# DeltaNet scan: one full product with zero-padded 128x128 q-k blocks in place of a pair of 64-column products

## The chip, the cores and the metric

The kernel runs on one core of a Trainium2 chip. The core has five engines with queues of their own: TensorE (PE in the profile, its weight loads PEld), VectorE (DVE), ScalarE (ACT), GpSimd (POOL) and SyncE (SP), which here only issues transfers. Each engine takes its instructions strictly in the order of its queue and waits at an instruction whose input or buffer isn't ready. Products land in PSUM, eight banks of 128 partitions x 512 fp32 numbers; all else lives in SBUF.

The metric is the device time of one execution in microseconds (us), smaller is better.

## What is computed

One layer of an encoder for two sequences with the same weights, 256 and 512 tokens, 1024 features, fp32 throughout. A modulated RMS norm gives `h`; one input projection feeds two mixers, neighbourhood attention with 8 heads of 64 and a gated DeltaNet with 4 heads of 128 that runs forward and backward; their outputs go through one output projection, then a second norm and a gated feed-forward with a convolution of width 3 follow. The change is in the DeltaNet, which works on chunks of 64 tokens:

```python
intra = jnp.where(causal, jnp.einsum('bhncd,bhnsd->bhncs', q, k) * decay, 0.0)
...
def step(S, xs):
    q_i, k_i, u_i, w_i, a_i, gl_i = xs
    v_new = u_i - jnp.einsum('bhcd,bhde->bhce', w_i, S)
    o = jnp.einsum('bhcd,bhde->bhce', q_i, S) + jnp.einsum('bhcs,bhse->bhce', a_i, v_new)
    S = S * jnp.exp(gl_i)[..., None, None] + jnp.einsum('bhcd,bhce->bhde', k_i, v_new)
    return S, o
```

`a_i` is `intra`, the masked 64x64 q-k matrix of a chunk; `a_i v_new` is the term that the change computes in another way.

## The kernel before

**Order of the work.** The kernel is traced as one long program of tiles. A framework then lays out the queue of every engine by priority (program order, with some parts raised) and by when it reckons that inputs and buffers are free, and it sets all waits. Tiles with the same tag share a fixed number of buffers (`bufs`); a tile whose buffer still has readers waits for them. So the order on an engine isn't written out by hand, and a change of buffers can change it.

**Stages.** The times are of the profiled execution. Norm and the first projections run up to about 73 us. The DeltaNet works on two pairs of heads (`hp` 0 and 1). For each pair there are projections (`dn_proj`, products on L476), the decay matrices (`dn_decay`: `rd` on L615 and L616, three products on L620, L621, a mask on POOL on L628), the q-k and k-k matrices (`dn_gram`), an inverse of 64x64 triangular blocks (`dn_solve`) and the scan (`dn_scan`). The first scan stands between 196 and 277 us, the second solve between 244 and 319, the second scan between 326 and 408. Beside the scans PE works off projections that don't depend on them: the second pair's, the gate `z` (both L476), and those of the attention (L868). The attention's core follows up to about 583, then the output projection, and from about 600 to the end the feed-forward, which neither uses nor feeds anything of the scan directly.

**Gram.** `dn_gram` writes the masked q-k matrices to `Ic` (L649), two 64x64 matrices for each pair of chunks: `[128, head, chunk pair, x, 64]`, rows 0 to 63 of one chunk, rows 64 to 127 of the other, one chunk of the forward and one of the backward direction.

**A step of the scan** (`step`, L752 to L806) does one chunk of both directions at once, for one head `j` and one sequence `s`. A scan has 8 + 4 steps in a row for two heads, 24 in all; the four rows (two heads, two sequences) are interleaved. One PSUM bank `B_` holds the three results of a step: `ps1` (256 columns), `ps2` and `ps4` (128 each). In order:

- L768: two products of `KQ` with the state `S` into `ps1`.
- L774 (DVE) makes the right side `r` of both halves, L781 (ACT) the part `tm` of the output. In the first step POOL copies `r` instead (L777).
- L782: the product with the inverse `Wbd` into `ps2`; this is `v_new`.
- L786 (DVE) and L788 (ACT) write scaled halves into `XS`.
- L790 (ACT), twice: each half of `ps2` is copied to its own 128-column part of `XB`, whose other rows are zero.
- L793: two products of `Kt` with `XS` into `ps1`; L796 (DVE) updates `S`.
- L802, twice: `Ic` (128 rows, 64 columns) times each part of `XB` into one half of the partitions of `ps4`.
- L806 (DVE) adds `tm` and writes the output over `Wbd`.

Instructions of different engines on the same PSUM bank are kept apart by waits, so L793, which writes the bank that L790 reads, comes after the copies.

**Other names that the steps below touch.** `MO` is a buffer of 6 KB a partition, used by constants at the start and by both solves (memset L657, copies L678, products L729, copies L735). `raw` (L875) holds the attention's queries or keys while they are normed (copies from PSUM L878, squares L884, a DVE chain from L885 to L888, transposes L894); it has one buffer, which `rd` shares. `zz` (L824) is a load into the buffer that the solve's products L729 read. The streams of the modulation use products with 32 columns (L192), and their weights go into `aw` and `au` (L502). `WRB` = 2 is the number of buffers for the loads of `w_o` (L1063). `vec` holds small per-feature vectors, among them the 176 columns for the feed-forward's convolution. L1224 are subtractions on POOL in the second norm.

Of the kernel before, what the change touches and what calls it, by code (L numbers as in the profile page):

```python
# [45 lines left out]
NV1 = VEC["n1g"][0]  # L46
NC1 = CST["bo"][0]
# [55 lines left out]
def layer(ctx: ExitStack, tc: tile.TileContext, I: dict, yout: bass.AP, dbg=None):  # L103
# [7 lines left out]
    vec = cpool.tile([P, VEC["_n"][1] - NV1], F32, name="vec")  # L111
# [3 lines left out]
    nc.sync.dma_start(vec[:], I["vec"][:, NV1:])  # L115
    nc.scalar.dma_start(cst[:], I["cst"][:, NC2:])

    vec2 = []

    def V(n, i=0, m=None):  # L120
        o, w = VEC[n]
        t_, o = (vec, o - NV1) if o >= NV1 else (vec2[0], o)
        return t_[:, o + i:o + (i + m if m is not None else w)]
# [14 lines left out]
    def load_w(pool, src, bufs, hp=HPW):  # L138
        """[128, 1024] weights -> (hi, lo)"""
# [11 lines left out]
    def rsqrt(out, v, shape, tag):  # L151
        """out = v ** -0.5 (v > 0), Newton on the integer seed"""
        a = small.tile(shape, F32, name="rs_a", tag="rs_a" + tag, bufs=2)
        ti = small.tile(shape, I32, name="rs_t", tag="rs_t" + tag, bufs=2)
# [23 lines left out]
    bw = cpool.tile([P, KD, 32], F32R, name="bw")  # L178
    braw = arow[:, 0:128].rearrange("p (k c) -> p k c", k=KD)
    nc.scalar.dma_start(braw, I["wba"])  # L180
    split(braw, bw[:, :, 0:16], bw[:, :, 16:32])

# [4 lines left out]
    def ada_piece(s, i, row, brow, load, PS, w4=None):  # L187
        """rows k = 4 i.. of set s; the four partial sums in rows 32 k.."""
        w4 = w4 or load(ada_src(s, i))
        p_ = PS()  # L190
        for kk in range(4):
            nc.tensor.matmul(p_[32 * kk:32 * kk + 32, :], cs[:, 4 * i + kk, :], w4[kk], start=True, stop=True)  # L192
        nc.vector.tensor_tensor(row[:], p_[:], row[:] if i else brow, ALU.add)
# [21 lines left out]
    def ada_ahead(sets, row, bias, load, PS):  # L215
        """each piece is loaded a step before it is used"""
# [24 lines left out]
    # ================= mixer =================  # L241
    with ExitStack() as mx:
# [20 lines left out]
        with tc.tile_pool(name="st", bufs=1, reuse_waits="tile") as st:  # L263
# [13 lines left out]
            # x, features on partitions  # L277
# [7 lines left out]
            # rstd of the tokens, along the free axis  # L285
# [50 lines left out]
            # the first four products run along with the rows of h  # L336
# [32 lines left out]
        at = px.enter_context(tc.tile_pool(name="at", bufs=1, side="right", reuse_waits="tile"))  # L369
# [14 lines left out]
        def gates_dn():  # L384
# [13 lines left out]
            ba = dn.tile([P, NT, 16], F32, name="ba")  # L398
# [3 lines left out]
            def to_slots(dst, src):  # L402
                """src [P, t, (d h)] -> dst [P, h, t', d]"""
# [10 lines left out]
            beta = dn.tile([P, 4, NT, 2], F32, name="beta")  # L414
            to_slots(beta, e1[:])
            y1 = dn.tile(sc8, F32, name="y1")
            nc.vector.tensor_tensor(y1[:], ba[:, :, 8:16], V("dtb").unsqueeze(1).broadcast_to(sc8), ALU.add)
            y2 = dn.tile(sc8, F32, name="y2")
# [4 lines left out]
            na = dn.tile([P, 8], F32, name="na")  # L423
            nc.scalar.activation(na[:], V("alog"), AF.Exp)
            nc.vector.scalar_tensor_tensor(y1[:], y1[:], -1.0, na[:].unsqueeze(1).broadcast_to(sc8), ALU.mult, ALU.mult)
            gg = dn.tile([P, 4, NT, 2], F32, name="gg")
# [16 lines left out]
            pdec = dn.tile(s48, F32, name="pdec")  # L443
# [18 lines left out]
        nc.gpsimd.memset(XB[:], 0.0)  # L462
# [21 lines left out]
        def ada_bufs():  # L484
            """buffers that the heads have left: five for weights, one for the bias row"""
# [3 lines left out]
            for tag, shape in (("dec", [P, 24, 64]), ("MO", [P, 12, P])):  # L489
                a_ = dn.tile(shape, F32, name="au", tag=tag)[:].rearrange("p a b -> p (a b)")  # L490
# [5 lines left out]
        def ada_load(src):  # L496
            """four k of a set"""
# [85 lines left out]
        def dn_scales(hp, sqs):  # L583
            # sums of squares: natural for k, swapped halves for q
# [6 lines left out]
            rkk = dn.tile([P, 2, NT], F32, name="rkk", tag="rkk", bufs=2)  # L591
# [40 lines left out]
        def dn_gram(hp, KQ, pp, dec, dv, SD):  # L632
            Ic = dn.tile([P, 2, NT, 2, 64], F32, name="Ic", tag="Ic", bufs=2)
            nc.vector.tensor_tensor(dec[:], dec[:], pp[:].rearrange("p h t d -> p (h t d)").unsqueeze(2).broadcast_to([P, 24, 64]), ALU.mult)
            dp = dec[:].rearrange("p (h t d) c -> p h t d c", h=2, t=NT)
            # Gram products
            for j in range(2):
                for b, n in SEQS:
# [6 lines left out]
                    for d in range(2):  # L645
                        ts_ = slice(0, n) if d == 0 else rev(0, n)
                        for e in range(2):
                            r_ = slice(e * 64, e * 64 + 64)
                            nc.vector.tensor_tensor(Ic[r_, j, b:b + n, e if d == 0 else 1 - e, :],  # L649
# [4 lines left out]
        def dn_solve(hp, Ic, dec, dv, SD):  # L654
            """operands [inverse of (1 + lower)] of every chunk; lhsT form, block-diagonal"""
# [23 lines left out]
            # one 32-block per partition (chunk, direction); upper form for both directions; its two blocks of 16  # L679
# [14 lines left out]
            # back to rows on partitions, as they are and transposed  # L694
# [9 lines left out]
            # blocks of 16 to blocks of 32  # L704
# [20 lines left out]
            def level(sel):  # L725
                """MO times the inverse (or its transpose), forward and backward"""
# [20 lines left out]
        def dn_scan(hp, KQ, Kt, Vt, pex, Ic, Wbd):  # L747
# [1 line left out]
            S = [[dn.tile([P, 2, P], F32, name=f"S{s}{j}", tag=f"S{s}{j}") for j in range(2)] for s in range(2)]  # L749
            half = lambda e: slice(e * 64, e * 64 + 64)  # L750

            def step(s, i, j):  # L752
# [8 lines left out]
                r = dn.tile([P, P], F32, name="r", tag="r", bufs=2)  # L761
                tm = dn.tile([P, P], F32, name="tm", tag="tm", bufs=2)
                xb = XB[:, j]
# [25 lines left out]
                for e in range(2):  # L789
                    nc.scalar.copy(xb[half(e), e, :], ps2[half(e)])  # L790
                if i < N - 1:
# [7 lines left out]
                    else:  # L799
                        nc.vector.tensor_copy(St[:].rearrange("p d c -> p (d c)"), ps1)  # L800
                for e in range(2):
                    nc.tensor.matmul(ps4[half(1 - e)], Ic[:, j, tp, x, :], xb[:, e, :], start=True, stop=True)  # L802
# [18 lines left out]
        def dn_final(hp, O, ssq):  # L821
# [1 line left out]
            zz = big.tile([P, 2, T], F32, name="zz", tag="sv")  # L823
            nc.sync.dma_start(zz[:], zd[2 * hp:2 * hp + 2].rearrange("h p t -> p h t"))  # L824
            so = dn.tile([P, 12], F32, name="so", tag="so")
            fo = dn.tile([P, 12], F32, name="fo", tag="fo")
# [31 lines left out]
        def att_proj(blk, evac):  # L858
            """token-major block of 256 columns; evac(psum tile with two token tiles, first t)"""
# [14 lines left out]
        def att_qk(hf, which, QT):  # L874
            raw = at.tile([P, NT, 4, 64], F32, name="raw", tag="raw", bufs=1)  # L875
# [4 lines left out]
            s_ = at.tile([P, 24], F32, name="s_", tag="s_")  # L880
            f_ = at.tile([P, 24], F32, name="f_", tag="f_")
            for i in range(24):
                jk = at.tile([P, 64], F32, name="jk", tag="jka", bufs=1)
# [35 lines left out]
        def att_core(hf, qk, SA, MX, units):  # L919
# [7 lines left out]
            # units of two query tiles: (query column, key blocks of kT, V tiles)  # L927
# [91 lines left out]

        def take(g, n):  # L1020
# [11 lines left out]
        pTs = [dn.tile([P, 512], F32, name="pT", tag=t)[:] for t in ("XS", "XB")]  # L1032
        scs = []
        for _ in range(2):
            sc3 = dn.tile([P, 3, 512], F32, name="sc", tag="Ic", bufs=2)
            scs.extend(sc3[:, u] for u in range(3))
# [43 lines left out]
        def proj(t, hd, pt, m, ks, tmp):  # L1080
            """X2 += gate * (rows ks of w_o)"""
# [9 lines left out]
        def proj_a():  # L1091
            """all but the last quarter of the mixer's columns"""
# [10 lines left out]
        def proj_b(t, raw, m, PS, tmp):  # L1103
            """the rest, the row's 1 / rms"""
# [31 lines left out]
    # ================= output projection, second norm =================  # L1136
    with ExitStack() as fx:
# [3 lines left out]
        dps = fx.enter_context(tc.tile_pool(name="dps", bufs=2, space=PSUM, reuse_waits="tile"))  # L1141
        h2hi = fp.tile([P, KD, T], F32R, name="h2hi")
# [231 lines left out]
```

## Time and profile before

| | |
|---|---|
| runs shown | 1191.91, 1193.77, 1193.95 us, median 1193.77 |
| profiled execution | span of 1191.6 us from the first to the last instruction, 17540 instructions; no time of its own is listed beside the span |
| mean granted TensorE clock | 0.981 |
| DVE, ACT, POOL busy | 726.8, 539.0, 69.0 us |
| DMA | 110.98 MB, mean 93 GB/s |
| L802, product `Ic` x `XB` | 192 weight loads of 136 ns and 192 product records of 273 ns (medians), from 200.4 to 407.2 us |
| L790, copies into `XB` | 96, median 261 ns |

An fp32 product appears as two records, one for each of its passes. A row of the timeline has its start, the time from its start to its end, engine, line, operation, what it writes and reads, the shape, how many instructions were merged, and in brackets the idle time before it and what ended that. "issue" is idle time in which the engine waited for nothing that the profile shows. Products overlap, so the busy time of PE is not the time for which it is held; for that the distances between starts are read.

### The profile page before, as it was taken

To read this page: it belongs to the slowest core of one execution; us is meant where nothing else is said; L and a number is where in the kernel's file an instruction comes from. 1 tells how busy PE (TensorE), PEld (TensorE's weight loads), DVE (VectorE), ACT (ScalarE), POOL (GpSimd) and SP (SyncE) were. 2 spreads that over 40 slices of the span, in tenths; PEclk is the share of its full clock that TensorE was granted. 3 is DMA by queue.
4 is the path that set the end of the run, shared out by engine and by line. 5 is a ranking of instruction groups with operands and counts; after the bars stand their busy time and mean duration, and the time that the engine had idled before them with its cause. 6 is when DMAs were issued, how large, how long until landed. Compare 5 with 4: busy or idle time off the path is not lost.

```text
span 1191.6 us, 17540 instructions
## 1 busy us (share of the span) xinstructions
PE 1150.3 (97%) x6682; PEld 940.3 (79%) x6682; DVE 726.8 (61%) x1544; ACT 539.0 (45%) x1301; POOL 69.0 (6%) x112
## 2 busy tenths in 40 slices
PE   6999899998999999999889999999999999999998
PEld 3778767777978698867678888888888888888886
DVE  5636986878476545364597655555655555564556
ACT  4357664574658666563476421430341233043310
POOL 1102103001100100100031000000000000000000
PEclk8999999999899999989999999999999999999999
DMA  8421142124241562281123411320311231031002
GB/s 306 197 71 36 54 142 90 58 94 142 73 149 55 176 231 72 76 264 60 59 75 106 142 54 29 113 66 6 115 63 36 71 89 53 18 102 58 19 1 106
DMA packets 43891, 110.98 MB, mean 93 GB/s; under 512 B 4384, under 2 KB 14528, under 8 KB 42528
## 3 DMA queue, kind: packets, MB, share of 16 engines
q1 hardware_dynamic: 36640, 92.93, 24.1%
q0 software_dynamic: 2928, 10.50, 2.7%
q10 hardware_dynamic: 4240, 6.44, 1.5%
q8 instruction: 52, 0.85, 0.3%
q14 instruction: 31, 0.25, 0.1%
HBM read 100.41 MB, written 9.45 MB: 92 GB/s over the span
## 4 chain that ended last, share of the span: by engine, by line
PE 79%; DVE 9%; ACT 7%; DMA 2%; issue 2%; SPq 0%; POOL 0%; DVEq 0%; ACTq 0%
PE dpt L1250 14%; PE upp L1169 10%; PE pjt L476 5%; PE pjt L868 4%; PE pat L1086 3%; PE sht L192 2%; PE pjt L345 2%; PE sdt L768 2%; ACT jk L884 1%; PE sdt L345 1%; PE sdt L944 1%; PE sdt L793 1%; PE sdt L802 1%; PE sdt L708 1%; PE mxt L970 1%
## 5 line engine op out<-in xcount | busy, mean ns | idle before, releaser
L136 DVE TENSOR_TENSOR wlo<-wraw,whi 128x1024 fp32r<-128x1024 f32 x72 | 88.1, 1223 | 115.9 <-ACT whi L135 115.7
L135 ACT CAST whi<-wraw 128x1024 fp32r<-128x1024 f32 x72 | 75.5, 1048 | 149.6 <-PE upp L1169 112.3
L1250 PE MATMUL dpt<-dh,gh 128*128 128x512 f32 x264 | 104.1, 395 | 0.2 <-DVE arow L1252 0.2
L1250 PE MATMUL dpt<-dl,gh 128*128 128x512 f32 x264 | 102.8, 389 | 0.0
L1250 PE MATMUL dpt<-dh,gl 128*128 128x512 f32 x264 | 102.3, 390 | 0.0
L1169 PE MATMUL upp<-h2lo,whi 128*128 128x256 f32 x352 | 99.8, 283 | 0.0
L1169 PE MATMUL upp<-h2hi,whi 128*128 128x256 f32 x352 | 98.8, 281 | 0.0
L1169 PE MATMUL upp<-h2hi,wlo 128*128 128x256 f32 x352 | 98.2, 279 | 0.0
L135 ACT CAST dh<-draw 128x1024 fp32r<-128x1024 f32 x22 | 23.1, 1052 | 160.4 <-PE dpt L1250 111.7
L1252 DVE TENSOR_TENSOR arow<-dpt,gb 128x512 f32<-128x512 f32 x72 | 49.8, 691 | 61.7 <-PE dpt L1250 59.6
L868 PE MATMUL pjt<-whi,hhi 128*128 128x256 f32 x288 | 85.4, 296 | 0.0
L868 PE MATMUL pjt<-whi,hlo 128*128 128x256 f32 x288 | 84.7, 294 | 0.0
L868 PE MATMUL pjt<-wlo,hhi 128*128 128x256 f32 x288 | 84.2, 292 | 0.0
L476 PE MATMUL pjt<-hhi,whi 128*128 128x512 f32 (+1 forms) x192 | 67.6, 352 | 1.3 <-DVE u L531 1.3
L476 PE MATMUL pjt<-hhi,wlo 128*128 128x512 f32 (+1 forms) x192 | 67.5, 353 | 0.0
L476 PE MATMUL pjt<-hlo,whi 128*128 128x512 f32 (+1 forms) x192 | 67.5, 352 | 0.0
L1169 PEld LDWEIGHTS upp<-h2hi,wlo 128*128 128x128 f32 x352 | 66.8, 190 | 0.2
L1169 PEld LDWEIGHTS upp<-h2hi,whi 128*128 128x128 f32 x352 | 66.3, 188 | 0.4
L1169 PEld LDWEIGHTS upp<-h2lo,whi 128*128 128x128 f32 x352 | 66.5, 189 | 0.0
L1250 PEld LDWEIGHTS dpt<-dh,gh 128*128 128x128 f32 x264 | 49.6, 188 | 13.4 <-DVE arow L1252 3.6
L868 PEld LDWEIGHTS pjt<-whi,hhi 128*128 128x128 f32 x288 | 55.9, 194 | 4.4 <-issue 3.6
L868 PEld LDWEIGHTS pjt<-whi,hlo 128*128 128x128 f32 x288 | 56.0, 195 | 2.5 <-issue 2.5
(910 smaller groups left out, 2882.7 us busy)
## 6 DMA issues: line engine op xcount, KB each, us to landing
wraw<-wup SPq DMA_DIRECT2D x44, 512.0 KB, 3.6
draw<-wdown SPq DMA_DIRECT2D x22, 512.0 KB, 3.5
araw<-ada SPq DMA_DIRECT2D x8, 1024.0 KB, 11.8
wraw<-wdn SPq DMA_DIRECT2D x16, 512.0 KB, 3.6
ew<-ada_w SPq DMA_DIRECT2D x16, 512.0 KB, 4.5
wraw<-wat SPq DMA_DIRECT2D x12, 512.0 KB, 4.1
sc<-abias POOLq DMA_DIRECT2D x24, 256.0 KB, 3.0
aw<-ada_w SPq DMA_DIRECT2D x10, 512.0 KB, 5.3
```

Of the source, the lines that this page charges most:

```text
L135: nc.scalar.copy(hi, src)
L136: nc.vector.tensor_tensor(lo, src, hi.bitcast(F32), ALU.subtract)
L192: nc.tensor.matmul(p_[32 * kk:32 * kk + 32, :], cs[:, 4 * i + kk, :], w4[kk], start=True, stop=True)
L345: nc.tensor.matmul(o_, w0[i][w][:, k * P:(k + 1) * P], m[:, k, c0:c1], start=(k == 0 and n == 0 and (c0 > 0 or i % 2 == 0)), stop=(k == KD ...
L476: nc.tensor.matmul(o_, w[:, k * P:(k + 1) * P], m[:, k, c0:c1], start=(k == 0 and n == 0), stop=(k == KD - 1 and n == 2))
L708: nc.tensor.matmul(ps[:, n * 32:n * 32 + 32], M16[:, n, :], R[:, n, :], start=True, stop=True)
L768: nc.tensor.matmul(ps1[:, d * P:(d + 1) * P], KQ[:, j, tl[d], 2 * pr[d]:2 * pr[d] + 2, :].rearrange("p b c -> p (b c)"), St[:, d, :], star ...
L868: nc.tensor.matmul(o_, a[:, k, t * P:(t + 1) * P], w[kh][m][:, kk * 256:(kk + 1) * 256], start=(k == 0 and n == 0 and t % 2 == 0), stop=(k ...
L1086: nc.tensor.matmul(pt[:], m[:, a, j, :], w[:, sl], start=(j == 0 and n == 0), stop=(j == len(ks) - 1 and n == 2))
L1169: nc.tensor.matmul(o_, (lo if n == 2 else hi)[:, k * P:(k + 1) * P], (h2lo if n == 1 else h2hi)[:, k, c0:c1], start=(k == 0 and n == 0), s ...
L1250: nc.tensor.matmul(ps[:], a[:, t * P:(t + 1) * P], m[:, sl], start=(i == 0 and n == 0), stop=(i == len(gs) - 1 and n == 2))
L1252: nc.vector.tensor_tensor(arow[:], ps[:], gb[:, grp(t), sl], ALU.mult)
```

## The change

`Ic` becomes `[128, head, chunk pair, x, 128]`: each 64x64 matrix stands in the columns of the other half, and the rest is zero, set by a memset on POOL for each pair of heads. `XB` goes. ACT copies the whole of `ps2` once, into `r`, and one product of 128 columns gives the whole of `ps4`. `r` has four buffers instead of two.

The two `Ic` buffers take 24 KB a partition instead of 12, and other tiles move for that: `rd` and `raw` go to `MO`'s buffer and the pool `at` goes; `S` is one tile; `bw` moves to `XS`'s buffer and is split later; small tiles share tags; the convolution's columns of `vec` are loaded later, as `vec3` on POOL's queue; `w_o`'s loads have one buffer of their own and the spare half (`rest[1]`) of the second attention bias tile, whose first counterpart (`rest[0]`) takes the fifth buffer of the modulation's stream, which was in `MO`. The loads of the mixer's rows before the second norm alternate between two pools with one buffer each. Comments were taken out; those lines are left out here.

```diff
+NV2 = VEC["fcw"][0]
...
-    vec = cpool.tile([P, VEC["_n"][1] - NV1], F32, name="vec")
+    vec = cpool.tile([P, NV2 - NV1], F32, name="vec")
...
+        bw = dn.tile([P, KD, 32], F32R, name="bw", tag="XS")
+        split(braw, bw[:, :, 0:16], bw[:, :, 16:32])
...
         XS = dn.tile([P, 2, 2, P], F32, name="XS", tag="XS")
         nc.gpsimd.memset(XS[:], 0.0)
-        XB = dn.tile([P, 2, 2, P], F32, name="XB", tag="XB")
-        nc.gpsimd.memset(XB[:], 0.0)
...
-            for tag, shape in (("dec", [P, 24, 64]), ("MO", [P, 12, P])):
-                a_ = dn.tile(shape, F32, name="au", tag=tag)[:].rearrange("p a b -> p (a b)")
+            for a_ in (dn.tile([P, 1536], F32, name="au", tag="dec"), rest[0]):
                 raws.append(a_[:, 0:1024].rearrange("p (k c) -> p k c", k=2))
...
-            rd = at.tile([P, 24, 64], F32, name="rd", tag="raw")
+            rd = dn.tile([P, 24, 64], F32, name="rd", tag="MO")
...
-            Ic = dn.tile([P, 2, NT, 2, 64], F32, name="Ic", tag="Ic", bufs=2)
+            Ic = dn.tile([P, 2, NT, 2, P], F32, name="Ic", tag="Ic", bufs=2)
+            nc.gpsimd.memset(Ic[:].rearrange("p h t x c -> p (h t x c)"), 0.0)
...
-                            nc.vector.tensor_tensor(Ic[r_, j, b:b + n, e if d == 0 else 1 - e, :],
+                            nc.vector.tensor_tensor(Ic[r_, j, b:b + n, e if d == 0 else 1 - e, (1 - e) * 64:(1 - e) * 64 + 64],
                                                     g4[r_, ts_, 1, :], dp[r_, j, b:b + n, d, :], ALU.mult)
...
-            S = [[dn.tile([P, 2, P], F32, name=f"S{s}{j}", tag=f"S{s}{j}") for j in range(2)] for s in range(2)]
+            S_ = dn.tile([P, 4, 2, P], F32, name="S", tag="S")
+            S = [[S_[:, 2 * s + j] for j in range(2)] for s in range(2)]
...
-                r = dn.tile([P, P], F32, name="r", tag="r", bufs=2)
+                r = dn.tile([P, P], F32, name="r", tag="r", bufs=4)
...
-                for e in range(2):
-                    nc.scalar.copy(xb[half(e), e, :], ps2[half(e)])
+                nc.scalar.copy(r[:], ps2)
...
-                for e in range(2):
-                    nc.tensor.matmul(ps4[half(1 - e)], Ic[:, j, tp, x, :], xb[:, e, :], start=True, stop=True)
+                nc.tensor.matmul(ps4, Ic[:, j, tp, x, :], r[:], start=True, stop=True)
...
-            raw = at.tile([P, NT, 4, 64], F32, name="raw", tag="raw", bufs=1)
+            raw = dn.tile([P, NT, 4, 64], F32, name="raw", tag="MO")
...
+        scs, rest = [], []
+        for i in range(2):
+            sc3 = dn.tile([P, 6, 512], F32, name="sc", tag="Ic", bufs=2)
+            scs.extend(sc3[:, u] for u in range(3))
+            rest.append(sc3[:, 3:6].rearrange("p a b -> p (a b)"))
...
-        pTs = [dn.tile([P, 512], F32, name="pT", tag=t)[:] for t in ("XS", "XB")]
+        pTs = [dn.tile([P, 512], F32, name="pT", tag=t)[:] for t in ("XS", "S")]
...
-                raw = wo.tile([P, D], F32, name="wraw", tag="wraw", bufs=WRB)[:]
+                raw = wo.tile([P, D], F32, name="wraw", tag="wraw")[:] if i % 2 else rest[1][:, 0:D]
...
+        vec3.append(fp.tile([P, VEC["_n"][1] - NV2], F32, name="vec3"))
+        nc.gpsimd.dma_start(vec3[0][:], I["vec"][:, NV2:])
...
-                    raw = wo.tile([P, KD, P], F32, name="mraw", tag="wraw", bufs=WRB)
+                    raw = (wo, wm)[t % 2].tile([P, KD, P], F32, name="mraw", tag="wraw")
```

More of the change, by code (lines that the diff above doesn't have):

```diff
@@ L114, in layer @@
     nc.sync.dma_start(cT[:], I["cT"])
-    nc.sync.dma_start(vec[:], I["vec"][:, NV1:])
+    nc.sync.dma_start(vec[:], I["vec"][:, NV1:NV2])
     nc.scalar.dma_start(cst[:], I["cst"][:, NC2:])
-    vec2 = []
+    vec2, vec3 = [], []
     def V(n, i=0, m=None):
         o, w = VEC[n]
-        t_, o = (vec, o - NV1) if o >= NV1 else (vec2[0], o)
+        t_, o = (vec3[0], o - NV2) if o >= NV2 else (vec, o - NV1) if o >= NV1 else (vec2[0], o)
         return t_[:, o + i:o + (i + m if m is not None else w)]
@@ L151, in rsqrt @@
     def rsqrt(out, v, shape, tag):
-        a = small.tile(shape, F32, name="rs_a", tag="rs_a" + tag, bufs=2)
-        ti = small.tile(shape, I32, name="rs_t", tag="rs_t" + tag, bufs=2)
+        a = small.tile(shape, F32, name="rs_a", tag="rs_a" + tag, bufs=1 if tag in ("6", "24") else 2)
+        ti = small.tile(shape, I32, name="rs_t", tag="rs_t" + tag, bufs=1 if tag in ("6", "24") else 2)
         nc.vector.tensor_scalar(ti[:], v.bitcast(I32), 1, None, ALU.logical_shift_right)
@@ L824, in dn_final @@
             nc.sync.dma_start(zz[:], zd[2 * hp:2 * hp + 2].rearrange("h p t -> p h t"))
-            so = dn.tile([P, 12], F32, name="so", tag="so")
-            fo = dn.tile([P, 12], F32, name="fo", tag="fo")
+            so = dn.tile([P, 12], F32, name="so", tag="ssk", bufs=2)
+            fo = dn.tile([P, 12], F32, name="fo", tag="rkk")
             for j in range(2):
@@ L1031, in layer @@
         att_half(0, iter(()), (0, 0, 0))
-        pTs = [dn.tile([P, 512], F32, name="pT", tag=t)[:] for t in ("XS", "XB")]
[L1033 to L1036, printed above, removed]
+        pTs = [dn.tile([P, 512], F32, name="pT", tag=t)[:] for t in ("XS", "S")]
         core = att_core(0, QT[0], SD, SD, [(a, b, u) for a in range(2) for b in range(2) for u in range(3)])
```

28 lines of the change are left out of this document (12 added, 16 removed).

## The prediction

> **What bounds the kernel now.** I read the page first, for the engines and the chain; then the windows that hold the two scans, the chain inside them, and the rows of TensorE around one scan step. On the page:
>
> ```profile
> PE 1150.3 (97%) x6682; PEld 940.3 (79%) x6682; DVE 726.8 (61%) x1544; ACT 539.0 (45%) x1301; POOL 69.0 (6%) x112
> ...
> PE 79%; DVE 9%; ACT 7%; DMA 2%; issue 2%; SPq 0%; POOL 0%; DVEq 0%; ACTq 0%
> ```
>
> TensorE (PE) carries 79% of the chain that ended last. Busy time alone would not prove that, because matmuls overlap. So, by stages: first scan, the second solve with no scan beside it, second scan.
>
> ```profile
> 195.00:278.00 83.00, 81.99 (x560) 59.62 (x560) 63.86 (x188) 54.75 (x154) 12.92 (x22) 1.00 0.24 77
> 278.00:325.00 47.00, 41.49 (x302) 40.20 (x301) 26.97 (x56) 26.82 (x96) 4.12 (x6) 0.89 0.33 114
> 325.00:408.00 83.00, 81.76 (x592) 60.24 (x590) 56.63 (x166) 53.65 (x190) 1.27 (x5) 1.00 0.32 105
> ```
>
> The columns are busy time of PE, weight load (PEld), DVE, ACT and POOL, then the granted clock. Both scans take 83 us with PE at a full clock and never long idle. The chain inside the two scans, by line:
>
> ```profile
> by line: PE pjt L476 26.9%; PE sdt L768 12.4%; PE sdt L793 9.9%; PE sdt L802 9.3%; PE sht L192 7.1%; PE sdt L782 7.0%; ACT XB L790 3.4%; PE sht L620 3.3%; DVE Vt L818 3.0%; ACT XS L788 2.5%; PE sht L642 2.3%; issue 2.2%; PE sht L205 1.9%; A
> ...
> by line: PE pjt L868 18.7%; PE sht L192 11.7%; PE sdt L768 9.4%; PE sdt L793 8.0%; PE sdt L782 7.9%; PE sdt L802 7.6%; ACT jk L884 7.1%; ACT tm L781 6.8%; ACT XB L790 4.0%; PE sht L199 2.9%; PE sht L894 2.8%; ACT whi L135 2.5%; issue 2.1%;
> ```
>
> The two operations that the change touches, L802 (the pair of 64-column products) and L790 (the copies that feed it), are both on the chain. The scan's products alternate with projections (L476, L868) that do not depend on them, so a shorter product lets the whole PE queue move up.
>
> **The change, part by part. The product.** The weight loads show how long PE is held:
>
> ```profile
> 384.60 0.30 PEld L768 LDWEIGHTS sdt<-S,KQ 128*128 128x128 f32 x2
> 384.82 0.30 PEld L782 LDWEIGHTS sdt<-r,Wbd 128*128 128x128 f32 x2
> 385.24 0.20 PEld L802 LDWEIGHTS sdt<-XB,Ic 128*64 128x64 f32 x4
> 385.61 0.30 PEld L768 LDWEIGHTS sdt<-S,KQ 128*128 128x128 f32 x2 [0.17 <-issue]
> ```
>
> An fp32 product leaves two records. A full one holds PE for 384.82 - 384.60 = 0.22 us. One full product and one pair take 385.61 - 384.82 = 0.79 us, so the pair costs 0.57 us: its own loads are short (four in 0.20 us, so the two halves do run side by side), but the product before it runs out first and the next load waits 0.17 us behind it. With all products full there is no such place, and I take 0.22: 0.35 us saved a step. How many steps:
>
> ```profile
> 195.00:258.00 63.00, 7.70 (x72) 3.89 (x72) 1.00 0.25 81
> 258.00:278.00 20.00, 2.73 (x26) 1.19 (x24) 1.00 0.20 65
> 325.00:408.00 83.00, 10.32 (x96) 4.76 (x96) 1.00 0.32 105
> ```
>
> These are L802's instructions alone, four loads a step: 18, 6 and 24, in all 48. The most that PE can save is 48 x 0.35 = 16.8 us. On the chain L802 has 9.3% and 7.6% of 83 us, 14.0 us; at 385.61 - 385.24 = 0.37 us a piece that is 38 steps, hence 38 x 0.35 = 13.3 us. I take off 1.0 for steps beside L192, whose blocks are narrow too and should keep part of the stop (an estimate: 3 steps' worth). I also take off the six steps of 258 to 278, 2.1 us: there the second solve already runs on DVE, and it, not PE, is late next.
>
> ```profile
> 259.64 2.02 DVE L680 STREAM_TRANSPOSE Wbd<-sv 128x1024 f32<-128x1024 f32 x1
> ```
>
> That leaves 10.2 us.
>
> The Trainium skill, page TensorEngine Tiling, section Overview, says that splitting the array for a stationary side of at most 64 columns gives up to twice the throughput; by it the pair costs no more than one product and this part saves nothing (the second rival). The same page, section Tiling Modes, says that changing the tiling mode drains the engine; the 0.17 us in front of L768 agrees with that.
>
> **The copies.**
>
> ```profile
> L790 ACT COPY XB<-sdt x96: 245/261/263, 197.5 to 406.6; 64x128 f32<-64x128 f32 x96
> ...
> L804 ACT COPY Wbd<-sdt x8: 247/266/266, 201.1 to 336.0; 128x128 f32<-128x128 f32 x8
> ...
> L793 PEld LDWEIGHTS sdt<-XS,Kt 128*128 128x128 f32 x160 | 21.5, 190 | 6.2 <-ACT XB L790 5.1 <-issue 0.2
> ```
>
> Two half copies of 0.261 become one of 128x128, for which L804 shows 0.266: 48 x 0.26 = 12.5 us less for ACT. Most is hidden. But L793 waits for the copies (5.1 us in the stretch of both scans), although it does not use them: it writes the bank that they read. L790 has 3.4% and 4.0% of the chain, 6.1 us; half of it, 3.1, is the second copy. Late next are PE's queue and L788, so I count 2.0. That copy now writes r, which the product L782 has just finished reading; r has four buffers instead of two, so nothing waits.
>
> **The zeros.** Two memsets of 128x3072 on POOL come in, one of 128x512 goes.
>
> ```profile
> 37.84 0.53 POOL L462 MEMSET XB<- 128x512 f32 x1
> 38.31 1.81 POOL L663 MEMSET Wbd<- 128x2048 f32 x1
> ...
> 43.35 0.16 POOL L668 MEMSET sv<- 128x32 f32 x1
> 106.33 1.38 POOL L657 MEMSET MO<- 128x1536 f32 x1 [62.82 <-PE sht L438]
> ...
> L649 DVE TENSOR_TENSOR Ic<-sdt,dec x16: 273/352/428, 125.6 to 136.1; 64x128 f32<-64x128 f32 x8, 64x256 f32<-64x256 f32 x8
> ```
>
> By 1.81 us for 2048 columns each takes 2.7 us. Both Ic buffers are free from the start and POOL idles 62.82 us before 106.33, as other early memsets show, so I take 0. Without that cover the first writer, L649 at 125.6, would wait up to 2.7 us, twice in all. The DVE writes keep their shapes.
>
> **rd and raw move into the buffer MO.** The second rd no longer runs early on DVE; it must wait until the first solve has left MO.
>
> ```profile
> 112.29 1.75 DVE L616 TENSOR_TENSOR rd<-cst,gcn 128x1536 f32<-128x1536 f32 x1
> ...
> 194.45 1.38 POOL L657 MEMSET MO<- 128x1536 f32 x1 [8.32 <-PE sdt L729]
> ...
> 196.56 0.51 DVE L786 TENSOR_TENSOR XS<-sdt,pex 64x128 f32<-64x128 f32 x2 [2.44 <-PE sdt L782]
> ...
> 233.92 1.06 POOL L678 COPY MO<-dec 32x384 f32<-32x384 f32 x2 [25.16 <-DVE dec L651]
> ```
>
> MO is free at 194.45; DVE then idles 2.44 us before 196.56, and 1.75 fits: 0. If DVE takes it behind the scan's first instructions, at most 1.75 us. At 112.29 DVE is relieved by the same 1.75, which I count as nothing. The memset of MO then goes behind rd's readers; L678, its first user, comes only at 233.92, with POOL idle 25.16 us before.
>
> The attention's raw is the risk. Its first copy runs beside the second solve, which needs MO to the end:
>
> ```profile
> 305.05 0.59 ACT L878 COPY raw<-pjt 128x512 f32<-128x512 f32 x1 [0.86 <-PE pjt L868]
> ...
> 311.95 0.95 ACT L735 COPY MO<-sdt 32x192 f32<-32x192 f32 x3 [3.64 <-PE sdt L729]
> ...
> 317.59 0.38 SPq L824 DMA_DIRECT2D zz<-zd  x1
> ...
> 327.47 0.36 ACT L788 ACTIVATE XS<-sdt,pex 64x128 f32<-64x128 f32 x1 [0.95 <-DVE XS L786]
> ...
> 342.94 0.38 PE L894 MATMUL sht<-cst,raw 128*128 128x128 f32 x2
> ...
> 358.15 0.59 ACT L878 COPY raw<-pjt 128x512 f32<-128x512 f32 x1
> ...
> 303.00:317.59 14.59, 2.80 (x16) 0.95 0.08 30
> ...
> 303.00:317.59 14.59, 1.17 (x2) 0.95 0.08 30
> ```
>
> The zz load shows that the solve's last products are done at 317.59 (it goes into the buffer that they read). raw's first copy therefore moves by 317.59 - 305.05 = 12.5 us. The last two rows are the squares L884 and the copies L878 before that moment, 2.80 + 1.17 = 4.0 us of ACT work, part of it in a stretch where ACT otherwise idles (3.64 us before 311.95). They move behind 317.59, at worst all into the second scan, which starts on ACT at 327.47; there ACT idles 83 - 53.65 = 29 us and is relieved of 24 x 0.26 = 6.2. The next use of raw, at 358.15, stands 15 us behind the last reader at 342.94. I take 1.0, bounds 0 and 12.5.
>
> **The rest.** The ada weights go into Ic's spare half instead of MO, free before the solve ends: 0, perhaps a gain. Two loads of w_o use the other spare half, so they still have two buffers. The feed-forward's vec3 is one more issue on POOL's queue ahead of the subtractions L1224:
>
> ```profile
> 599.38 1.97 POOL L1224 TENSOR_TENSOR h2lo<-h,h2hi 128x128 fp32r<-128x128 f32 x1 [43.07 <-DVE h L1223]
> ```
>
> POOL idles 43.07 us there: 0, at worst the issue itself. bw's split and the small tiles in shared tags are reused long after their last readers: 0. Orders will shift, as the framework lays out the queues anew; from nothing in the trace can I give that a sign, so it only widens the range.
>
> **Sum.** 10.2 + 2.0 - 1.0 = 11.2 us. The profiled execution has a span of 1191.6 us; the runs shown are 1191.91 to 1193.95 with median 1193.77, so 0.3 to 2.4 us lie around the span or between executions, untouched by the change. Span 1180.4, time 1193.8 - 11.2 = 1182.6 us.
>
> **The rivals.** First, slower: raw's 12.5 us are passed on whole. The three projection tiles wait for raw's copies, the keys' copies wait for the queries' transposes, PE runs out of projections in the second scan, and that scan gains nothing. The first scan's gain is then some 18 x 0.35 = 6.3 less 1.0: 1193.8 + 12.5 - 5.3 = 1201.0. It decides once the queries are more than the 15 us late that the row at 358.15 leaves. Against it: ACT has only 4.0 us more to do there, and room for it. Second, no change: the halves overlap, as the four loads in 0.20 us show, and the stops around them stay as waits for the copy; only ACT's 2.0 are won: 1191.8. Against it: the 0.17 us is put down to issue, not to another engine. Third, a smaller gain: the scans' own recurrence, DVE and ACT (63.86 and 54.75 of 83 us busy), is late next, and half of the PE gain comes back as waits: 5.1 + 2.0 - 1.0 = 6.1, 1187.7.
>
> **How the numbers follow.** Forecast 0.70, smaller gain 0.11, no change 0.07, slower 0.12. A measurement here tells 0.2%, 2.4 us, from no change; below 1191.4 are the first two: faster 0.81, same 0.07, slower 0.12. The low end is all of PE's and ACT's part, 16.8 + 3.1 = 19.9: 1174. The high end takes in the case of no change with 2.2 us of the unhidden zeros or rd: 1194. It leaves out the slower rival and little else.
>
> **What would show it.** Right: L802 with half its records, as 128*128 with no issue gap around it, a step between full products 0.22 longer, not 0.57; both scan windows some 4 to 6 us shorter; L790's count halved and L793's wait near 3 us. Wrong: L802 gone from the chain but the scans still 83 us; L878 waiting for L729 and PE for raw or QT; POOL's Ic memsets late and L649 behind them.

## The result and the profile after

The changed kernel took 1231.01 us (median; 1229.87 to 1233.13), the kernel before 1193.86 beside it: a ratio of 1.0312, 95% interval 1.0289 to 1.0334. It is 37 us slower where 11 us faster were forecast. The profiled execution has a span of 1231.2 us.

The windows of the prediction, taken of the changed kernel, and below them two narrower ones (columns as before: PE, PEld, DVE, ACT, POOL, granted clock, DMA share, GB/s):

```profile
195.00:278.00 83.00, 81.63 (x549) 64.82 (x550) 65.03 (x180) 50.95 (x138) 13.14 (x22) 1.00 0.21 66
278.00:325.00 47.00, 38.16 (x246) 37.59 (x245) 28.36 (x64) 16.46 (x49) 4.42 (x7) 0.74 0.33 105
325.00:408.00 83.00, 63.37 (x424) 54.85 (x422) 49.66 (x154) 45.47 (x159) 3.18 (x6) 0.89 0.24 83
...
380.00:395.00 15.00, 8.91 (x55) 6.85 (x54) 9.51 (x29) 6.91 (x23) 0.00 (x0) 1.00 0.01 1
395.00:420.00 25.00, 6.44 (x23) 4.22 (x24) 12.44 (x39) 15.41 (x78) 3.18 (x6) 0.52 0.40 147
```

The first window is as full as before. In the second PE has 246 product records where it had 302, in the third 424 where it had 592, and from 395 to 420 us it is busy for 6.44 of 25 us. What is missing is the work beside the scan. PE's timeline at the end of the second scan:

```profile
393.67 0.49 PE L782 MATMUL sdt<-r,Wbd 128*128 128x128 f32 x2 [1.58 <-ACT tm L781]
394.51 0.49 PE L800 MATMUL sdt<-r,Ic 128*128 128x128 f32 x2 [0.35 <-ACT r L789]
401.79 3.41 PE L840 MATMUL sdt<-cst,Vt 128*128 128x128 f32 x11 [6.79 <-ACT Vt L835]
...
416.64 1.97 PE L892 MATMUL sht<-cst,raw 128*128 128x128 f32 x8 [10.66 <-DVE raw L886]
...
420.46 2.78 PE L191 MATMUL sht<-aw,cs 128*32 128x512 f32 x10
```

The scan itself became shorter: from its first to its last L782 in this view it takes 60.5 us (333.4 to 393.9), before 80.0 (326.0 to 406.0). Behind it PE waits 6.79 us and 10.66 us, and only at 420 us do the modulation's rows (L191, before L192) start, which the kernel before began inside the scan, at 346.7 us. The chain of work in order of time (its longest pieces) names what PE waits for:

```profile
398.38 0.41 ACT jk L828 x2
401.64 3.02 ACT Vt L835 x10
405.05 0.41 ACT Vt L835
405.50 0.49 PE sdt L840
406.02 0.89 DVE zz L843 x2
414.83 1.77 DVE raw L886
416.64 1.56 PE sht L892 x6
```

L828 is `dn_final`'s sum of squares for the second pair of heads, L886 the norm of the attention's queries: two computations with no data in common. ACT's timeline shows how they touch:

```profile
398.38 0.31 ACT L828 ACTIVATE jk<-Vt 128x128 f32<-128x128 f32 x1
...
398.81 0.26 ACT L882 ACTIVATE jk<-raw 128x64 f32<-128x64 f32 x1
```

The queries' first square (L882) starts right after the last square of `dn_final`, and both write a tile named `jk`, a scratch tile that nobody reads. In the kernel before, the attention's `jk` had a tag of its own in the pool `at`; the change put it under the tag `jk` of the other pool, with one buffer for all. Buffers of a tag are handed out in the order of the program, and `dn_final(1)` stands ahead of the attention there. The rows of the squares, in the kernel before and in the changed one, have the start of the first and of the last behind the durations:

```profile
L884 ACT ACTIVATE jk<-raw x96: 240/257/260, 305.7 to 479.8; 128x64 f32<-128x64 f32 x96
...
L882 ACT ACTIVATE jk<-raw x96: 238/256/279, 398.8 to 517.2; 128x64 f32<-128x64 f32 x96
```

The changed instructions are as forecast. The weight loads of one step (to be held against the rows from 384.60 in the prediction), and the rows by line from 195 to 410 us:

```profile
384.60 0.30 PEld L768 LDWEIGHTS sdt<-S,KQ 128*128 128x128 f32 x2 [0.69 <-DVE S L795]
384.81 0.30 PEld L782 LDWEIGHTS sdt<-r,Wbd 128*128 128x128 f32 x2
385.04 0.30 PEld L800 LDWEIGHTS sdt<-r,Ic 128*128 128x128 f32 x2
385.26 0.30 PEld L768 LDWEIGHTS sdt<-S,KQ 128*128 128x128 f32 x2
```

```profile
L792 PEld LDWEIGHTS sdt<-XS,Kt 128*128 128x128 f32 x160 | 21.1, 190 | 9.9 <-ACT r L789 8.0 <-ACT whi L136 0.8 <-issue 0.2
...
L800 PEld LDWEIGHTS sdt<-r,Ic 128*128 128x128 f32 x96 | 14.9, 190 | 3.8 <-ACT r L789 1.2 <-issue 0.8 <-DVE XS L786 0.5
...
L789 ACT COPY r<-sdt 128x128 f32<-128x128 f32 x48 | 12.5, 260 | 3.4 <-PE sdt L782 3.1
```

From L782 to the next L768 it is 0.45 us instead of 0.79, with 0.22 for the new product.

### The profile page after: what moved, and what is told of

Read it like the earlier page. It is cut to its first block, busy times and chain, and to the rows that moved or that the text cites. A ratio compares the mean times of both kernels' runs of the same rounds, so it can differ in the third digit from the quotient of the medians.

```text
span 1231.2 us, 17297 instructions
## 1 busy us (share of the span) xinstructions
PE 1155.2 (94%) x6586; PEld 951.3 (77%) x6586; DVE 728.4 (59%) x1544; ACT 528.9 (43%) x1255; POOL 70.2 (6%) x114
## 3 DMA queue, kind: packets, MB, share of 16 engines
q10 hardware_dynamic: 4240, 6.44, 1.4%
## 4 chain that ended last, share of the span: by engine, by line
PE 76%; DVE 9%; ACT 8%; DMA 4%; issue 3%; SPq 0%; POOL 0%; ACTq 0%; DVEq 0%; POOLq 0%
PE dpt L1252 13%; PE upp L1171 10%; PE pjt L866 5%; PE pjt L475 3%; PE pat L1086 3%; PE sht L191 2%; PE pjt L344 2%; ACT jk L882 1%; PE dpt L1086 1%; PE sdt L792 1%; PE sdt L344 1%; PE sdt L942 1%; PE sdt L729 1%; PE sdt L768 1%; PE sdt L708 1%
## 5 line engine op out<-in xcount | busy, mean ns | idle before, releaser
L866 PEld LDWEIGHTS pjt<-wlo,hhi 128*128 128x128 f32 x288 | 56.5, 196 | 1.7 <-issue 1.7
```

Source lines behind the costliest of these rows:

```text
L866: nc.tensor.matmul(o_, a[:, k, t * P:(t + 1) * P], w[kh][m][:, kk * 256:(kk + 1) * 256], start=(k == 0 and n == 0 and t % 2 == 0), stop=(k ...
```

## The experiments

Three theories stood at the start. **A**: the shared scratch tile holds the queries' squares until the second scan has ended, and with them `raw`, the keys' copies, the projection tiles and the modulation's rows, so that PE has nothing to put between the scan's steps. **B**: `raw` in `MO`'s buffer does that, the prediction's slower rival. **C**: the product, the copy or the zeros cost the time.

| kernel | what | median us | ratio to before, 95% interval |
|---|---|---|---|
| e1 | after, own scratch tile | 1198.65 | 1.0030, 1.0011 to 1.0049 |
| e2 | before, shared scratch tile | 1233.92 | 1.0325, 1.0285 to 1.0366 |
| e3b | before, rd and raw in MO | 1204.57 | 1.0087, 1.0052 to 1.0122 |
| e4 | e1 with the pair of products | 1209.30 | 1.0119, 1.0083 to 1.0156 |
| e5 | before, rd in MO | 1197.94 | 1.0030, 1.0016 to 1.0043 |
| e6 | e1, raw out of MO | 1189.29 | 0.9956, 0.9938 to 0.9973 |
| e7 | e6, rd out of MO | 1191.20 | 0.9983, 0.9960 to 1.0006 |
| e8 | e7 with half copies | 1200.67 | 1.0049, 1.0032 to 1.0067 |
| e9 | e7 with half copies and pair | 1201.71 | 1.0057, 1.0035 to 1.0078 |
| e10 | e7 with the pair | 1199.09 | 1.0031, 1.0013 to 1.0048 |
| e11 | after, raw out of MO | 1229.12 | 1.0289, 1.0270 to 1.0307 |

The kernel before had medians of 1195.05 (e1 to e4), 1194.99 (e5 to e8) and 1195.24 us (e9 to e11). Where two kernels are compared, their ratios are, at 1195 us for 1. A ratio need not be the quotient of the two medians: e7's twelve runs spread from 1189.0 to 1201.7 us, and the quotient of its medians is 0.9968 where its ratio is 0.9983.

**e1: the scratch tile apart.** `cst3` is a tile of constants that the second solve reads last.

```diff
-        cst3 = dn.tile([P, NC2 - NC1], F32, name="cst3")
+        cst3 = dn.tile([P, NC2 - NC1], F32, name="cst3", tag="cst3")
...
-                jk = dn.tile([P, 64], F32, name="jk", tag="jk", bufs=1)
+                jk = dn.tile([P, 64], F32, name="jk", tag="cst3")
```

> The kernel after, with the junk tile of the attention's squares (L882) taken out of the tag that it shares with the junk tile of dn_final's squares (L828): it takes the place of the constants cst3 instead, whose last reader is the second solve. Nothing else differs. Theory A (the shared junk tile holds the queries' squares until dn_final of the second scan at 398 us, and with them raw, the keys' copies, the projections and the rows of ada, so that PE runs out of filler after about 368 us): the queries' squares come at 315 to 335 us as in the kernel before, the ada rows are back inside the second scan, and the time falls from 1231 to 1180-1197 us. Theory B (raw in MO's buffer, which waits for the second solve and delays the first copy of raw from 305 to 326 us): the first copy stays at 326 us and the time stays within 5 us of 1231. Theory C (the new product, the single copy or the zeros cost the time): stays at 1231.

1198.65 us: 2.82%, or 33.7 us, went with one tag. The line of the squares and the third window of e1:

```profile
L882 ACT ACTIVATE jk<-raw x96: 239/257/280, 328.0 to 483.1; 128x64 f32<-128x64 f32 x96
```

```profile
325.00:408.00 83.00, 81.60 (x587) 68.63 (x587) 58.30 (x169) 57.65 (x222) 3.17 (x6) 0.96 0.31 104
```

The squares start at 328.0 us instead of 398.8, and PE is full again beside the second scan. The median is 1.7 us above the range that was given; against the kernel before a small loss remains.

**e2: the same tile shared in the kernel before.**

```diff
-                jk = at.tile([P, 64], F32, name="jk", tag="jka", bufs=1)
+                jk = dn.tile([P, 64], F32, name="jk", tag="jk", bufs=1)
```

> The kernel before, with the junk tile of the attention's squares (L884) put under the tag of dn_final's squares (L830), one buffer for both; product, copies, zeros and all other buffers stay as they were. Theory A: the time rises from 1194 to 1220-1240 us, the queries' squares come only behind dn_final's of the second scan (after 410 us). Theories B and C: 1194 us within 3 us.

This one line makes the kernel before 3.25% slower, 39 us, as much as the whole change lost. Its squares start at 401.6 us (behind 410 was expected), and its third window is as empty as that of the changed kernel:

```profile
L884 ACT ACTIVATE jk<-raw x96: 238/256/279, 401.6 to 518.6; 128x64 f32<-128x64 f32 x96
```

```profile
325.00:408.00 83.00, 68.51 (x405) 52.59 (x403) 45.33 (x141) 44.82 (x158) 3.17 (x6) 0.72 0.15 52
```

With e1 and e2 theory A is shown from both sides; B and C as the main cause have fallen.

**e3b and e5: rd and raw in MO, in the kernel before.** In e3b both move; the modulation's weights that were in `MO` take `raw`'s old place. e5 moves `rd` alone.

```diff
...
-            rd = at.tile([P, 24, 64], F32, name="rd", tag="raw")
+            rd = dn.tile([P, 24, 64], F32, name="rd", tag="MO")
...
-            raw = at.tile([P, NT, 4, 64], F32, name="raw", tag="raw", bufs=1)
+            raw = dn.tile([P, NT, 4, 64], F32, name="raw", tag="MO")
```

> The kernel before, with rd and raw in the buffer of the tag MO, as in the kernel after; the weights of ada that were in MO (au) take the old place of raw instead. The junk tile keeps its own buffer. Theory A: the first copy of raw moves from 305 to about 318-326 us and the time stays between 1192 and 1203 us (the prediction's own bound was 1201 when the delay is passed on whole). Theory B: about 1225-1231 us. Theory C: 1194 us.

> The kernel before with rd alone moved to the buffer of the tag MO; raw keeps its own. It splits the 9.5 us that rd and raw in MO cost together. Theory R1 (rd is the costly one: the zeroing of MO on POOL now waits for rd's readers and stands ahead of the masks of dec, so ACT's exponential of dec runs at 127 us instead of 119, the first Gram products come 7 us later, and rd of the second pair waits for the first solve): 1200 to 1206 us, with the first Gram products at 132 us and the second scan starting at 331 to 336 us. Theory R2 (raw is the costly one, because its first copy waits for the second solve): 1193 to 1197 us.

Both moves cost 0.87%, 10.4 us, and at 1204.57 e3b lies above the range of theory A; `rd` alone costs 0.30%, 3.6 us, less than R1 asked for and just over R2. So `raw` has some 6.8 us of it. The first copies of `raw`, e3b and then e5:

```profile
L878 ACT COPY raw<-pjt x12: 567/586/606, 329.5 to 484.7; 128x512 f32<-128x512 f32 x12
```

```profile
L878 ACT COPY raw<-pjt x12: 565/586/592, 291.9 to 476.3; 128x512 f32<-128x512 f32 x12
```

`rd` acts by a way that the prediction had not looked at. POOL and ACT in e5, then the same ACT instruction in the kernel before:

```profile
111.82 1.38 POOL L657 MEMSET MO<- 128x1536 f32 x1 [68.20 <-PE sdt L620]
113.24 0.90 POOL L628 TENSOR_SCALAR_AFFINE_SELECT dec<-dec 64x768 f32<-64x768 f32 x1
```

```profile
125.13 0.85 ACT L548 ACTIVATE KQ<-u 128x768 f32<-128x768 f32 x1
...
126.57 1.28 ACT L629 ACT_TABLE_LOAD   x1
127.86 1.49 ACT L629 ACTIVATE dec<-dec 128x1536 f32<-128x1536 f32 x1
```

```profile
118.66 1.49 ACT L629 ACTIVATE dec<-dec 128x1536 f32<-128x1536 f32 x1
```

The zeroing of `MO` (at 106.33 us before) now waits for `rd`'s reader L620 and stands on POOL ahead of the masks L628. The framework laid the exponential L629, which needs the masks, behind a SiLU on ACT, and ACT has 14 table loads where it had 12, each of 1.28 us. The masks themselves end no later (at 117.0 us, before at 117.7), so what moved is the order on ACT. The exponential ran 9 us later, and the first write of the masked q-k matrices (L649) came 7 us later, at 133.0 us instead of 125.6. The expectation calls this the first Gram products; the first of these products start at 111.7 us, as before.

Most of the delay is made up ahead of the first scan, whose first L782 starts at 197.5 us (before 196.1). The second scan starts at 331.9 us (before 326.0) and ends at 408.6 (before 406.0). The second pair's `rd` (L616) now runs at 197.5 us, ahead of the first scan's L786. Which of these the 3.6 us come from was not separated.

**e4: the pair of products in e1.**

```diff
-                nc.tensor.matmul(ps4, Ic[:, j, tp, x, :], r[:], start=True, stop=True)
+                for e in range(2):
+                    nc.tensor.matmul(ps4[half(1 - e)], Ic[:, j, tp, x, (1 - e) * 64:(1 - e) * 64 + 64], r[:], start=True, stop=True)
```

> e1 with the full product of a step (L800) replaced by two products of 64 columns on the two column halves of the same blocks, both with the full r as moving operand; copies, zeros and buffers are those of e1. It prices the shape of the product alone. The prediction took 0.35 us a step for 38 steps on the chain, less some neighbours, 10.2 us: then e4 is 7 to 14 us over e1. If column tiles cost the same as full products, e4 is within 2 us of e1.

0.89% over e1, 10.6 us. The loads of e4 around one pair, and of e1 around one full product, each among projections:

```profile
348.83 0.19 PEld L867 LDWEIGHTS pjt<-wlo,hhi 128*128 128x128 f32 x1
349.15 0.20 PEld L801 LDWEIGHTS sdt<-r,Ic 128*64 128x64 f32 x4
349.52 0.19 PEld L867 LDWEIGHTS pjt<-whi,hhi 128*128 128x128 f32 x1 [0.17 <-issue]
```

```profile
348.68 0.19 PEld L866 LDWEIGHTS pjt<-whi,hlo 128*128 128x128 f32 x1
348.80 0.31 PEld L800 LDWEIGHTS sdt<-r,Ic 128*128 128x128 f32 x2
349.03 0.19 PEld L866 LDWEIGHTS pjt<-wlo,hhi 128*128 128x128 f32 x1
```

From projection to projection it is 0.69 us with the pair and 0.35 with the full product: 0.34 us a step, where the prediction had 0.35. The two are typical: the medians of all such places are 0.69 us in e4 (14 places) and 0.35 in e1 (18).

**e6 and e11: raw out of MO.** In e6, on top of e1, `raw` takes the spare half of the first `Ic` buffer, free since the first scan, and the modulation's weights that were there go to `MO`. e11 has this edit alone: the scratch tile stays shared.

```diff
-            for a_ in (dn.tile([P, 1536], F32, name="au", tag="dec"), rest[0]):
+            for a_ in [dn.tile([P, 1536], F32, name="au", tag=t) for t in ("dec", "MO")]:
...
-            raw = dn.tile([P, NT, 4, 64], F32, name="raw", tag="MO")
+            raw = rest[0].rearrange("p (t h c) -> p t h c", t=NT, h=4)
```

> e1 (the kernel after with the junk tile apart) with raw in the spare half of the first Ic buffer, free since the end of the first scan, and the weights of ada (au) that were there in MO. rd stays in MO. Theory R1: 1194 to 1200 us, little under e1's 1198.7, though raw's first copy comes before the second solve's end. Theory R2: 1186 to 1192 us.

> The kernel after with its shared junk tile kept, and raw in the spare half of the first Ic buffer (au in MO), as in e6. Raw's place was worth 9.4 us with the junk tile apart (e1 to e6). If the junk tile alone ends the wait of the queries' squares, raw's place is worth nothing here: 1228 to 1233 us, with the squares still at 395 us or later. If the two waits add up: 1220 to 1224 us.

e6 is 0.74% under e1, 8.8 us, as R2 had it, and it is the version that beats both kernels: 0.9956 of the kernel before, a gain of 5.3 us where 11 were forecast. `raw`'s first copy in e6 (its tile is now part of `sc`), and in e11 the first copy and the squares:

```profile
L876 ACT COPY sc<-pjt x12: 563/584/591, 292.5 to 468.1; 128x512 f32<-128x512 f32 x12
```

```profile
L876 ACT COPY sc<-pjt x12: 563/586/595, 291.5 to 506.7; 128x512 f32<-128x512 f32 x12
```

```profile
L882 ACT ACTIVATE jk<-sc x96: 240/256/269, 395.2 to 512.0; 128x64 f32<-128x64 f32 x96
```

In e11 the copy is as early as in e6, and the squares still wait until 395 us: it gains 0.23%, 2.7 us, on the changed kernel, a difference inside the two intervals. The later wait hides the earlier one.

**e7 to e10: the square of product and copies.** e7 is e6 with `rd` in the second `Ic` buffer, which is zeroed only after `rd`'s readers. e8 halves the copies again, e10 brings back e4's pair, e9 both.

```diff
-            rd = dn.tile([P, 24, 64], F32, name="rd", tag="MO")
+            rd = Ics[1][:].rearrange("p h t x c -> p (h t x c)")[:, hp * 1536:hp * 1536 + 1536].rearrange("p (n c) -> p n c", n=24)
...
-            Ic = dn.tile([P, 2, NT, 2, P], F32, name="Ic", tag="Ic", bufs=2)
+            Ic = Ics[hp]
...
+        Ics = [dn.tile([P, 2, NT, 2, P], F32, name="Ic", tag="Ic", bufs=2) for _ in range(2)]
```

```diff
-                nc.scalar.copy(r[:], ps2)
+                for e in range(2):
+                    nc.scalar.copy(r[half(e)], ps2[half(e)])
```

> e6 with rd in the second Ic buffer, which is zeroed only after rd's readers; so the product of the change stays whole, and junk tile, raw and rd are all free of the waits that the change brought. If junk tile, rd and raw are the whole of what was lost: 1182 to 1190 us, some 8 to 11 us under the kernel before, as the product alone gave (e4 less e1: 10.6 us), with the first Gram products back at 125 us. If another move (ba, y1, y2, bw, vec3, the shared small tiles, the zeros on POOL) also costs: 1190 to 1197 us.

> e7 with the one ACT copy of ps2 into r replaced by two copies of 64 rows. It prices the halving of the copies. The prediction counted 2.0 us for 48 copies fewer: then e8 is 1 to 4 us over e7. If ACT's copies are hidden in the scan: within 1 us of e7. If each costs its 0.26 us on the chain of 38 steps: 10 us over.

> e7 with the pair of 64-column products of e4, and one copy as in e7. It is the fourth corner of the square of e7, e8 and e9. If the savings add up: 1199 to 1204 us, as e4 stood to e1. If they overlap: within 5 us of e7's 1191.

> e8 with the pair of 64-column products of e4: product and copies are as costly as in the kernel before, but buffers, zeros and small tiles are those of e7, free of the three waits. If the savings of product (10.6 us) and copies (9.5 us) add up, e9 is 1208 to 1214 us, and the other moves of the change would then cost some 16 us against the kernel before. If they overlap (PE is full in this stretch, and what is saved in one place is waited for in the other), e9 is 1195 to 1204 us and the other moves cost little.

e7, at 1191.20, lies in its second range, 1.2 us above the first. Its first write of `Ic` is at 123.0 us, 10 us earlier than in e6, and it is no faster, so it isn't shown that this delay is what costs the 3.6 us of e5. In ratios the pair costs 0.48%, 5.7 us, with one copy (e10) and 0.08% with two (e8 to e9, intervals overlap); the second copy 0.66%, 7.9 us, with the full product (e8, where 1 to 4 us were expected) and 0.26% with the pair (e10 to e9, intervals overlap); both together 0.74%, 8.8 us. Together they are thus less than the sum of the two single effects, 13.6 us, which speaks for an overlap: what the one leaves, the other takes. But the 4.8 us between the two figures are no more than the widths of the four intervals leave open (an estimate from them), and e10's median, 1199.09, lies just in the range that stood for adding up.

In the profiled executions, what e7 saves in the scans isn't all kept: its second scan ends 13.0 us earlier than in the kernel before (393.0 against 406.0), the first product of the attention's core (L942, before L944) comes 6.1 us earlier (431.9 against 438.0). The stretch of its second scan holds 500 product records, that of the kernel before 570. The halved products are 48 of the difference; the other 22 are work that no longer stands beside the scan, and between scan and core stand 271 records where there were 254. The loads of L792 (L793) in the stretch of both scans, of e7 and of e8:

```profile
L792 PEld LDWEIGHTS sdt<-XS,Kt 128*128 128x128 f32 x160 | 21.6, 190 | 7.0 <-ACT r L789 3.9 <-issue 2.0
```

```profile
L793 PEld LDWEIGHTS sdt<-XS,Kt 128*128 128x128 f32 x160 | 21.2, 190 | 8.7 <-ACT r L790 6.8 <-ACT jk L883 0.9 <-issue 0.3
```

The wait for the copies grows from 3.9 to 6.8 us with the second copy; it is the wait that the prediction read in the kernel before (5.1). The 2.9 us are less than the 7.9 (0.66%) between the two times; where the rest goes was not separated, as the queues are laid out anew in each kernel.

## Why the prediction was wrong

Step by step along the ratios, from before to after: product and copies as before in the new buffers without the three waits +6.8 us (e9), product and copies changed -8.8 (e7), `rd` into `MO` -3.2 (e6, unclear, the intervals overlap), `raw` into `MO` +8.8 (e1), the scratch tile shared +33.7 (after). Together +37.3.

- **The step that failed** is in "The rest": "the small tiles in shared tags are reused long after their last readers: 0". It asked when the buffer's former users are done by the trace of before, and overlooked that the queries' squares run, in time, ahead of `dn_final(1)`, which is the former user in the order of the program. e1 and e2 give this term 34 to 39 us.
- **The product**, 10.2 us: right in kind, and the price of a step was right (0.34 us against 0.35). What it is worth depends on what stands around it: 10.6 us in e1 (e4), 5.7 in e7 (e10), 1.0 beside half copies (e8 to e9). The agreement of 10.6 with 10.2 is partly luck. The Trainium skill, page TensorEngine Tiling (Array Packing), section Overview, gives up to twice the throughput for tiles of at most 64 columns. These steps don't reach it: the pair takes 0.69 us against 0.35 between the same neighbours. The same page of the Trainium skill says in Tiling Modes that a change of mode drains the engine; the 0.17 us of idle time behind the pair agrees with it.
- **The copies**, 2.0 us: too small with the full product (7.9); with the pair it is 3.1, which the intervals don't tell from 2.0 or from nothing. The sum of product and copies, 12.2, was measured as 8.8 together.
- **The zeros**, 0: right; both memsets run at 2.7 us each long before the first write of `Ic` (132.2 us), as POOL's rows in the changed kernel show.

```profile
58.55 2.67 POOL L633 MEMSET Ic<- 128x3072 f32 x1 [27.77 <-DVE hlo L333]
...
64.58 2.67 POOL L633 MEMSET Ic<- 128x3072 f32 x1
```

- **rd**, 0: mis-sized, 3.6 us in e5 (with the buffers of e6 it can't be told from nothing: e6 to e7). Of POOL's queue the step looked at L678, 120 us later, and not at L628, the instruction right behind the moved memset, nor at what the framework then does with ACT's order.
- **raw**, 1.0 out of 0 to 12.5: mis-sized, 6.8 us (e5 to e3b) and 8.8 us (e6 to e1). The slower rival described this mechanism and gave 1201.0; e1, which has it without the shared tile, took 1198.65. That the two are so close is partly luck, as by the sum above e1 also holds e9's open 6.8 us. The forecast should have stood nearer to that end.
- Of the signs named, the halved records, the 0.22 us and the halved copies came. L792's wait for the copy was 8.0 us instead of 3; in e7, where PE has work between the steps, it is 3.9. Of the signs for "wrong", PE waiting for `raw` came (10.66 us at 416.64), as the slower rival had it, but from the shared scratch tile and not from `MO`: e2, with `raw` in its old buffer, shows the same loss.

What stays open is e9's +6.8 us: the other moves (`bw`, the small tiles of the gates, `r`'s buffers, `vec3`, the zeros) were not tried one by one. The two profiled executions, 7.6 us apart, show where it lies:

| stretch, from the first product of a stage to that of the next | before | e9 |
|---|---|---|
| start to the attention's core (L944) | 438.0 us | 439.8 us |
| attention's core to `w_o` | 85.4 us | 88.3 us |
| `w_o` to the feed-forward | 105.7 us | 108.7 us |

So up to the attention only 1.8 us are lost. In the core PE waits 2.24 us for the norm of `raw` (L888) at 455 us, where the kernel before waits 0.58, and the granted clock is 0.83 from 450 to 460 us (1.00 at the same place before, 448 to 458); the last stretch has such a dip too (below). Whether the other moves bring these on isn't shown.

## What to carry to other kernels

A scratch tile that nobody reads still orders its writers: one buffer under one tag ties two independent computations together in the order of the program, whatever the order in time. So for each tile that a change puts under a shared tag, list its users in the order of the program, and ask of each pair whether the later one runs earlier today. And before an instruction on the critical path is made cheaper, look for the filler that keeps the engine busy around it: here losing the filler cost three times what the cheaper instruction could bring.

## What was not expected of the hardware

The stretch from the first product of `w_o` to the first of the feed-forward, the same work in all kernels, took 105 to 106 us in the profiled executions of the kernel before, e3b and e4, and 107 to 109 us in the others. Ten microseconds in the middle of it, in the kernel before and in e9:

```profile
593.00:603.00 10.00, 7.77 (x41) 5.94 (x41) 9.35 (x25) 6.93 (x14) 2.42 (x2) 1.00 0.69 211
```

```profile
598.00:608.00 10.00, 8.02 (x33) 5.91 (x34) 8.23 (x24) 5.29 (x11) 0.51 (x1) 0.83 0.43 120
```

At the same place in the work the granted clock was 1.00 in one and 0.83 in the other, with PE no less busy. The kernels with the dip take 1 to 3 us longer here, as much as the smaller effects in the table, so nothing under 3 us is read from one pair of kernels. The new buffers for the loads of `w_o` don't decide it: e5, with the old ones, has the dip (0.84), and e4, with the new ones, doesn't. What decides it was not found. A long gap shows more plainly: 0.52 in the changed kernel from 395 to 420 us, with PE busy for 6.44 of 25 us. The Trainium skill, page TensorE: Matmul & The Clock Gate, Part 1, says that the gate follows how busy PE has been and passes half of the pulses when it has idled; the 0.52 agrees.
